# A hybrid attention layer on one core: sums of squares later, latent products earlier, the output product one block ahead

## The chip, the cores and the metric

The kernel runs on one core of one Trainium2 chip. The metric is the device time of one execution in microseconds (us), lower is better. TensorE (PE in the rows) does matmuls and transposes, with its weight loads apart (PEld); VectorE is DVE, ScalarE is ACT, GpSimd is POOL, and SyncE (SP) issues the DMAs.

## The reference, cut to what matters

```python
n = rms_norm(x, norm_g)                     # x: 2048 positions x 1024
dq, dk, dv, dgate, cq, ckv, kr, mgate = split(n @ w_in)
# group A: 4 heads, two softmax maps each
od = softmax(q1 k1) v - lam * softmax(q2 k2) v
od = rms_norm(od, subln_g) * (1 - lam_init) * silu(dgate)
# group B: 8 latent heads
q = rms_norm(cq, g) @ w_uq ; k, v = split(rms_norm(ckv, g) @ w_ukv)
om = causal_attention([q, rope], [k, rope], v) * silu(mgate)
h = x + concat(od, om) @ w_out
h = h + (p @ w_ple) * sigmoid(h @ w_ple_gate)
out = rms_norm(h, final_norm_g)
```

All inputs are float32, attention is causal, and rotary embedding is applied to parts of queries and keys.

## The kernel before, in words

Positions go in 16 blocks of 128 (`NB`) and 4 groups of 512 (`t`, `NT`). A float32 operand is split into two fp32r parts, high and low, and each product is three matmuls (high x high, high x low, low x high), so one 128-position block times 512 columns over a depth of 1024 is 24 matmuls. Work is written down by loops and reordered on each engine by a scheduler, with tile pools whose few buffers decide when a writer must wait. There are four stages.

**Input projection.** `load_x` (L213 and on) brings one of 8 row pieces of x for a group of 512 positions into a raw buffer (3 of them, shared with the weights), ScalarE writes the high part `xh` and the square `s1`, VectorE the low part `xl`, and GpSimd adds the squares into `sq` (the square of piece 0 writes it, L223; one buffer for all groups). `norms(t)` multiplies `sq` by ones into `pn` (8 small matmuls, L259), from which the scale `r_all` comes. The first pass over the 16 blocks makes the gates of group B: `mm_s` is the block's 24 matmuls into one of five PSUM tiles `ps`, `gate_evac` applies silu with the scale on ScalarE and stores the block. In block 0 of each group of four `norms` comes first, and the x of the next group is loaded two pieces per block.

**Latents.** `latent(b)` makes the 512 latent columns of a block, `turn` transposes them (`tpc`) into `cT`, and `up(t)` gives 12 products for a group of 512 positions: keys (3 matmuls), queries (9) and values (3) for each of four head pairs, 48 in all. Each is split by ScalarE and VectorE into one quarter of a ring `stage` and stored (128 x 1024 numbers) to `k_s`, `q_s` or `v_s`; the ring has four quarters, so a split waits until the store four products back has landed. From the ninth step on, each step of the loop does three products; what is left after the last step follows with two maxima of scores (`prep`, L171) for every product. The keys, values and queries of the first head pair are loaded back at named places of this loop, and the maxima need them.

**Latent attention, then differential attention.** The second has 4 heads x 8 pairs of blocks. `block` makes scores and exponentials (`pu`, `pb`), `weigh` transposes probabilities (one PSUM buffer `tpa`), ScalarE copies them (`ah`), they are multiplied by the values (`pod`), normed (`otd`), transposed and stored. Its loads (`load_out`) bring the output weights in pieces of 128 x 256, each with a cast on ScalarE and a subtraction on VectorE.

**Output.** For block b, from 15 down to 0: `mix` loads the gated attention `zg` (two loads and the gates, multiplied on GpSimd), `transpose_split` transposes and splits it (`zt4`), `p1` is the product with the output weights (48 matmuls), added to x; `p3` is the embedding product (12 matmuls); the sum is transposed (`ht4`) and multiplied by the gate weights into `p2` (48 matmuls). `load_split` brings the gate and embedding weights through two buffers `wr` at the start of this stage.

Of the kernel before, what the change touches and what calls it, by code (L numbers as in the profile page):

```python
# [8 lines left out]
F32 = mybir.dt.float32  # L9
F32R = mybir.dt.float32r  # L10
# [8 lines left out]
P = 128  # L19
S = 2048  # L20
D = 1024
KT = D // P
# [42 lines left out]
def tile_hymba(ctx, tc, a, out):  # L65
# [130 lines left out]
    with ExitStack() as c1:  # L196
# [138 lines left out]
        def gate_evac(b, pt, c0, w, g0):  # L335
            gt = ev.tile([P, 512], F32, name="gt", tag="e")
            A.activation(gt[:, :w], pt[:, c0:c0 + w], AF.Silu, scale=r_all[:, b:b + 1])
            nc.sync.dma_start(out=gate_s[b][:, g0:g0 + w], in_=gt[:, :w])

        for b in range(NB):  # L340
            if b == 3 * NB // 4:
                wn = load_w(1024, 512)
            pt = mm_s(b, *wg, 512)
            if b % 4 == 0:
                norms(b // 4)
            gate_evac(b, pt, 0, 512, 0)
# [205 lines left out]

            return [lambda pr=pr, f=f: f(pr) for pr in range(4) for f in (keys, queries, values)]

        turned, fresh, ups = 0, [], []
        for b in range(NB + 3):
            n = min(b, NB, max(0, 2 * (b - 3)))
            if b < NB:
                latent(b)
            for x in sorted(qns):  # L560
                q_turn(x)
            for x in fresh:
                q_rotary(x)
            fresh = list(range(turned, n))
            for x in fresh:
                turn(x)
            n_up = 3 if b >= 8 else 0
            for f in ups[:n_up]:
                f()
            if b in (12, 16):  # L570
                pair0[0].pop(0)()
            if b == NB:
                q0 = xpool.tile([P, 2, 2, 2, 512], F32R, name="q0", tag="vbig", bufs=2)
                for t in range(2):
                    load_q(0, t, q0[:, t])
                    maxes += [f for x in prep(0, t) for _, _, f in x]
                pair0[1].pop(0)()
                pair0[1].pop(0)()
            ups = ups[n_up:] + [f for t in range(turned // 4, n // 4) for f in up(t)]
            turned = n  # L580
        for i, f in enumerate(ups):
            f()
            for g in maxes[:2]:
                g()
            maxes = maxes[2:]
            if len(ups) - 1 - i == 12:
                pair0[0].pop(0)()
                pair0[1].pop(0)()
            if len(ups) - 1 - i == 9:
                pair0[0].pop(0)()  # L590
        for g in maxes:
            g()
        pair0[1].pop(0)()
# [214 lines left out]


    SC_D = 64.0 ** -0.5  # L810
    with ExitStack() as c3:
        sm = c3.enter_context(tc.tile_pool(name="p3m", bufs=4, reuse_waits="tile"))
        sb = c3.enter_context(tc.tile_pool(name="p3s", bufs=2, reuse_waits="tile"))
# [10 lines left out]
        def load_out():  # L824
# [13 lines left out]

            return [(0.3, lambda n=n: piece(n)) for n in range(4 * KT)]

        probs = {}

        def block(h, b):
# [8 lines left out]
            def unit(m, u):  # L852
                hd = heads[h]
                if m == 0 and u == 0:
                    st["s"] = sm.tile([P, 2, 2], F32, name="ssum", tag="ssum", bufs=4)
                if u == 0:
                    st[m] = pp.tile([P, S], F32, name="pb", tag=f"pb{m}", bufs=(6 if m == 0 else 2))
# [115 lines left out]
        for i, (h, g) in enumerate(order):  # L973
            if i % 8 == 0 and h < 3:
                pending = load_head(h + 1)
            if h == 3:
                pending, wload = pending + wload[:WN], wload[WN:]
            n = -(-len(pending) // max(1, HE - i % 8)) if h < 3 else len(pending)
            ld, pending = pending[:n], pending[n:]
            nxt = [x for y in blocks[LEAD + 2 * i:LEAD + 2 * i + 2] for x in block(*y)]  # L980
            if i == len(order) - 2:
# [3 lines left out]
            merge([(c, lambda x=(c, f): both.append(x)) for c, f in weigh(h, g)],  # L985
                  [(c, lambda x=(c, f): both.append(x)) for c, f in ld])
            merge(both, nxt)


    with ExitStack() as c4:  # L990
# [8 lines left out]
        turned = xpool.tile([P, 2, KT, P], F32R, name="turned", tag="vbig", bufs=2)  # L999
        wg, wl = [[], []], [[], []]  # L1000
        for k in range(KT):
            if k % 2 == 0:
                tg = dict(tag="vbig", bufs=2) if k >= 4 else dict(tag="big")
                w = xpool.tile([P, 2, 2, D], F32R, name="wg", **tg)
            for i in range(2):
                wg[i].append(w[:, k % 2, i])
        for i in range(2):
            for k in range(2):
                wl[i].append(wp.tile([P, D], F32R, name=f"wl{i}{k}"))

        def load_split(hi, lo, src, kts):
            for k in range(kts):
# [16 lines left out]
            return hi, lo  # L1029

        def product(pt, xh_, xl_, wh, wl, kts, nc_=2):
            for c in range(nc_):
                sl = slice(c * D // nc_, (c + 1) * D // nc_)
                for k in range(kts):
# [4 lines left out]
        st = {}  # L1039

        def load_mix(b):
            if b == NB - 1:
                zg = mixed[:, 0]
            else:
                zg = sb.tile([P, D], F32, name="zg", tag="zg")
                mix(b, zg, sb.tile([P, D], F32, name="gt4", tag="gt4", bufs=1))
            xr = sb.tile([P, D], F32, name="xr4", tag="xr4")
            nc.sync.dma_start(out=xr, in_=a["x"][b * P:(b + 1) * P, :])
            pr = sb.tile([P, 2, P], F32, name="pr4", tag="pr4", bufs=1)
            nc.sync.dma_start(out=pr, in_=a["pT"][:, b * P:(b + 1) * P].rearrange("(k p) s -> p k s", p=P))  # L1050
            ph = rp.tile([P, 2, P], F32R, name="ph4", tag="ph4")
            pl = rp.tile([P, 2, P], F32R, name="pl4", tag="pl4")
            V.tensor_copy(ph, pr)
            V.tensor_sub(pl, pr, ph.bitcast(F32))
            st[b] = zg, xr, ph, pl

        zh, zl = transpose_split(mixed[:, 0], "zt4", 2, (turned[:, 0], turned[:, 1]))
        load_mix(NB - 1)
        load_split(*wl, a["w_ple"], 2)
        load_split(*wg, a["w_gate"], KT)  # L1060
        nc.sync.dma_start(out=fg, in_=a["final_g"].partition_broadcast(P))
        for b in reversed(range(NB)):
            zg, xr, ph, pl = st.pop(b)
            if b > 0:
                load_mix(b - 1)
            p1 = ps.tile([P, D], F32, name="p1", tag="p4")
            product(p1, zh, zl, *wo, KT)
            for c in range(2):
                sl = slice(c * 512, (c + 1) * 512)
                V.tensor_add(xr[:, sl], p1[:, sl], xr[:, sl])  # L1070
            if b > 0:
                zh, zl = transpose_split(st[b - 1][0], "zt4", 2)
            p3 = ps.tile([P, D], F32, name="p3", tag="p4")
            product(p3, ph, pl, *wl, 2)
# [3 lines left out]
            product(p2, hh, hl, *wg, KT, parts)  # L1078
            sg4 = rg.tile([P, D], F32, name="sg4", tag="sg4")
            s4 = sb.tile([P, 4], F32, name="s44", tag="s44")  # L1080
            for c in range(parts):
# [60 lines left out]
```

## Time and profile before

| | |
|---|---|
| median of 3 runs | 2037.75 us (2037.64 to 2038.78) |
| the profiled execution | 2036.48 us, span 2034.7 us, mean granted TensorE clock 0.983 |
| TensorE busy | 1923.8 us (95%) |
| VectorE, ScalarE, GpSimd busy | 1223.9 (60%), 919.8 (45%), 503.9 us (25%) |
| first pass, latents, latent attention, differential attention, output (us of the span) | to 114, to 690, to 1155, to 1570, to 2035 |

TensorE is the engine that is nearly always busy; a busy share is an average over stages. The granted clock is 1.00 at 2.4 GHz and 0.5 at 1.2 GHz, so a stretch with 0.75 is half at one and half at the other. The first column of a timeline is the start in us from the span's start, the second the duration; matmuls overlap their neighbours, so their distance is read from starts.

### The profile page before, as it was taken

To read this page: it belongs to the slowest core of one execution; us is meant where nothing else is said; L and a number is where in the kernel's file an instruction comes from. 1 tells how busy PE (TensorE), PEld (TensorE's weight loads), DVE (VectorE), ACT (ScalarE), POOL (GpSimd) and SP (SyncE) were. 2 spreads that over 40 slices of the span, in tenths; PEclk is the share of its full clock that TensorE was granted. 3 is DMA by queue.
4 is the path that set the end of the run, shared out by engine and by line. 5 is a ranking of instruction groups with operands and counts; after the bars stand their busy time and mean duration, and the time that the engine had idled before them with its cause. 6 is when DMAs were issued, how large, how long until landed. Compare 5 with 4: busy or idle time off the path is not lost.

```text
span 2034.7 us, 28244 instructions
## 1 busy us (share of the span) xinstructions
PE 1923.8 (95%) x9521; PEld 1518.9 (75%) x9521; DVE 1223.9 (60%) x2749; ACT 919.8 (45%) x2089; POOL 503.9 (25%) x464
## 2 busy tenths in 40 slices
PE   8999999999999699999999989998988899999997
PEld 5788878898887477777777667776766687777786
DVE  5353677632446487888888688777886523333322
ACT  4422101122333467677767676777786311111111
POOL 4400345300000166666656400000011201111100
PEclk9999999999998899999999999999999999999999
DMA  5442333322167643524141311531022522222210
GB/s 166 140 149 87 130 126 135 120 87 77 63 209 254 225 129 105 142 55 131 36 109 51 93 43 39 151 113 33 16 81 78 185 90 68 88 88 88 76 47 21
DMA packets 171681, 209.74 MB, mean 103 GB/s; under 512 B 38876, under 2 KB 99180, under 8 KB 171536
## 3 DMA queue, kind: packets, MB, share of 16 engines
q1 hardware_dynamic: 171536, 207.93, 32.7%
q8 instruction: 75, 1.23, 0.3%
q14 instruction: 70, 0.57, 0.1%
HBM read 129.65 MB, written 78.14 MB: 102 GB/s over the span
## 4 chain that ended last, share of the span: by engine, by line
PE 76%; DVE 7%; ACT 7%; DMA 4%; issue 2%; POOL 2%; SPq 1%; ACTq 0%; POOLq 0%; DVEq 0%
PE p L1035 6%; PE p L1037 6%; PE p L1036 6%; PE ps L252 5%; PE ps L253 5%; PE ps L251 5%; PE pod L936 3%; PE pm L171 3%; PE po L704 3%; PE pst L675 3%; PE po L705 3%; PE pst L673 3%; PE pst L674 3%; PE ps L372 3%; PE ps L370 3%; PE ps L371 3%
## 5 line engine op out<-in xcount | busy, mean ns | idle before, releaser
L690 POOL TENSOR_TENSOR acc<-ph,acc 128x512 f32<-128x512 f32 (+3 forms) x208 | 216.7, 1042 | 164.5 <-DVE acc L685 75.8
L251 PE MATMUL ps<-wh,xh 128*128 128x512 f32 (+1 forms) x640 | 229.5, 359 | 9.3 <-DVE wh L240 8.2
L252 PE MATMUL ps<-wl,xh 128*128 128x512 f32 (+1 forms) x640 | 227.8, 357 | 0.5 <-DVE wl L241 0.4
L253 PE MATMUL ps<-wh,xl 128*128 128x512 f32 (+1 forms) x640 | 227.2, 357 | 0.4 <-DVE xl L228 0.3
L678 ACT ACTIVATE ph<-pst 128x512 fp32r<-128x512 f32 (+1 forms) x320 | 170.3, 532 | 114.1 <-PE pst L675 61.9
L695 DVE TENSOR_TENSOR pl<-pst,ph 128x512 fp32r<-128x512 f32 (+1 forms) x320 | 193.3, 607 | 45.6 <-ACT pst L679 42.8
L107 POOL TENSOR_TENSOR s<-s,half 128x2 f32<-128x2 f32 (+1 forms) x48 | 31.9, 664 | 648.2 <-DVE s L106 552.5
L872 DVE TENSOR_REDUCE mxd<-pu 128x1 f32<-128x1024 f32 (+4 forms) x192 | 173.0, 909 | 21.7 <-PE pu L871 14.8
L883 ACT ACTIVATE pb<-pu,nm 128x1024 f32<-128x1024 f32 (+4 forms) x192 | 165.3, 866 | 27.2 <-DVE nm L878 16.9
L679 ACT ACTIVATE pst<-pst 128x512 f32<-128x512 f32 (+1 forms) x320 | 168.9, 528 | 0.0
L868 PE MATMUL pu<-hd 128*128 128x512 f32 (+3 forms) x320 | 141.3, 442 | 21.2 <-ACT pb L883 19.1
L251 PEld LDWEIGHTS ps<-wh,xh 128*128 128x128 f32 x640 | 121.6, 190 | 29.6 <-ACT sq L223 6.5
L936 PE MATMUL pod<-ah,hd 128*128 128x256 f32 (+1 forms) x576 | 141.6, 370 | 0.5 <-ACT ah L928 0.5
L173 DVE TENSOR_REDUCE mx<-pm 128x1 f32<-128x512 f32 x192 | 130.0, 680 | 15.1 <-PE pm L171 15.0
L253 PEld LDWEIGHTS ps<-wh,xl 128*128 128x128 f32 x640 | 121.7, 190 | 19.7 <-DVE xl L228 2.0
L252 PEld LDWEIGHTS ps<-wl,xh 128*128 128x128 f32 x640 | 121.7, 190 | 19.0 <-DVE wl L241 1.6
L1084 DVE TENSOR_TENSOR sg<-p,sg 128x512 f32<-128x512 f32 (+1 forms) x34 | 20.8, 655 | 175.5 <-ACT sg L1083 175.5
L704 PE MATMUL po<-ph,vall 128*128 128x512 f32 (+1 forms) x320 | 117.8, 374 | 4.2 <-ACT ph L678 4.0
L869 PE MATMUL pu<-hd 128*128 128x512 f32 (+3 forms) x320 | 121.7, 386 | 0.0
L673 PE MATMUL pst<-QH,kall 97*128 97x512 f32 (+2 forms) x296 | 119.1, 402 | 0.0
L171 PE MATMUL pm<-kall,QH 96*128 96x512 f32 (+3 forms) x296 | 115.2, 404 | 3.9 <-DVE mx L173 2.5
L705 PE MATMUL po<-pl,vall 128*65 128x512 f32 (+1 forms) x320 | 115.4, 363 | 0.0
(263 smaller groups left out, 4620.8 us busy)
## 6 DMA issues: line engine op xcount, KB each, us to landing
hd<-dq_s SPq DMA_DIRECT2D x192, 128.0 KB
wr<-in_w_in SPq DMA_DIRECT2D x40, 256.0 KB
xr<-in_xT SPq DMA_DIRECT2D x32, 256.0 KB
dq_s<-th SPq DMA_DIRECT2D x32, 256.0 KB
dq_s<-tl SPq DMA_DIRECT2D x32, 256.0 KB
k_s<-stage SPq DMA_DIRECT2D x16, 512.0 KB
q_s<-stage SPq DMA_DIRECT2D x16, 512.0 KB
v_s<-stage SPq DMA_DIRECT2D x16, 512.0 KB
```

Of the source, the lines that this page charges most:

```text
L171: T.matmul(pm[:, :w], lhsT=q, rhs=keys_of(pr, e, c)[0][0:96, :w], start=True, stop=True)
L251: T.matmul(pt[:, :w], lhsT=h, rhs=wh[k][:, :w], start=(k == 0), stop=False)
L252: T.matmul(pt[:, :w], lhsT=h, rhs=wl[k][:, :w], start=False, stop=False)
L253: T.matmul(pt[:, :w], lhsT=l, rhs=wh[k][:, :w], start=False, stop=(k == KT - 1))
L673: T.matmul(pt[:, o:], lhsT=kh[0:97], rhs=qh[0:97, o:], start=True, stop=False)
L678: A.activation(ph[:, o:], pt[:, o:], AF.Exp, scale=SC_M)
L690: eng.tensor_add(self.acc[:, o:], ph[:, o:].bitcast(F32), self.acc[:, o:])
L695: V.tensor_sub(pl[:, o:], pt[:, o:], ph[:, o:].bitcast(F32))
L704: T.matmul(self.po[:, o:], lhsT=vv[:, 0:128], rhs=ph[:, o:], start=(kc == 0), stop=(kc == self.n - 1))
L705: T.matmul(self.po2[:65, o:], lhsT=vv[:, 64:129], rhs=pl[:, o:], start=(kc == 0), stop=False)
L872: V.reduce_max(st["x", m][:, u:u + 1], pu[:, :w], axis=AX.X)
L936: T.matmul(st["po"][:, o:], lhsT=vv, rhs=st[u][:, i, o:], start=(kc == 0), stop=(kc == nk - 1))
```

## The change

First pass: `norms` moves from the first to the third block of each group, and the products of three blocks are held in PSUM until then, to be evacuated together. Latents: four products per step from the seventh step on, in place of three from the ninth, with the loads of the first pair by a count of products, and three maxima per product. Differential stage: the rows of x of the last block, its gated attention and that of block 14 are brought in, transposed there (`turn_z`), the last block's output product (`top_part`, 48 matmuls) is made in the score tiles, and half of the gate weights are loaded in 16 pieces of 128 x 256 (`load_gate`); the `pb` buffers of map 0 go from 6 to 5. Output: the output product of a block is made one block earlier (`add_z`), and only the other half of the gate weights is loaded in this stage.

```diff
+        held = []
         for b in range(NB):
...
-            pt = mm_s(b, *wg, 512)
-            if b % 4 == 0:
+            held.append((b, mm_s(b, *wg, 512)))
+            if b % 4 == 2:
                 norms(b // 4)
-            gate_evac(b, pt, 0, 512, 0)
+            if b % 4 >= 2:
+                for x, pt in held:
+                    gate_evac(x, pt, 0, 512, 0)
+                held = []
...
+        def run_up():
+            nonlocal done
+            ups.pop(0)()
+            done += 1
+            if done == 27:
+                pair0[0].pop(0)()
+            if done == 38:
+                pair0[1].pop(0)()
+            if done == 39:
+                pair0[0].pop(0)()
+            for g in maxes[:3]:
+                g()
+            del maxes[:3]
...
-            n_up = 3 if b >= 8 else 0
-            for f in ups[:n_up]:
-                f()
-            if b in (12, 16):
-                pair0[0].pop(0)()
...
+            for _ in range(min(len(ups), 4 if b >= 6 else 0)):
+                run_up()
+            if b in (12, 14):
+                pair0[0].pop(0)()
...
+        while ups:
+            run_up()
...
+        def load_gate(k2):
...
+                nc.sync.dma_start(out=ws, in_=a["w_gate"][(2 * k2 + k) * P:(2 * k2 + k + 1) * P, sl])
+                A.copy(w[:, k, 0, sl], ws)
+                V.tensor_sub(w[:, k, 1, sl], ws, w[:, k, 0, sl].bitcast(F32))
...
+        def turn_z(b, g, to):
+            tp = ps_t.tile([P, 4, P], F32, name="tpz", tag="tpa")
+            for j in range(4):
+                k = 4 * g + j
+                T.transpose(tp[:, j], side["zg", b][:, 0, k * P:(k + 1) * P], ident)
+            split_ps(to[:, 0, 4 * g:4 * g + 4], to[:, 1, 4 * g:4 * g + 4], tp)
+
+        def top_part(c, k0, n):
...
+                T.matmul(o, lhsT=z[:, 0, k], rhs=wh, start=(k == 0), stop=False)
+                T.matmul(o, lhsT=z[:, 0, k], rhs=wl, start=False, stop=False)
+                T.matmul(o, lhsT=z[:, 1, k], rhs=wh, start=False, stop=(k == KT - 1))
+            if k0 + n == KT:
+                V.tensor_add(top[:, sl], o, top[:, sl])
...
+            if i == len(order) - 5:
+                lay(NB - 1, top)
+            if i == len(order) - 4:
+                turned = make_z()
+                side["z"] = turned[:, 0]
+                more = [(0.45, lambda g=g: turn_z(NB - 1, g, turned[:, 0])) for g in range(2)]
+            if i == len(order) - 3:
+                lay(NB - 2, None)
+                more = [(1.4, lambda k=k: top_part(0, k, 2)) for k in range(0, KT, 2)]
             if i == len(order) - 2:
-                mixed = xpool.tile([P, 2, D], F32, name="mixed", tag="vbig", bufs=2)
-                mix(NB - 1, mixed[:, 0], mixed[:, 1])
+                pending = pending + load_gate(0) + load_gate(2)
+                more = [(1.4, lambda k=k: top_part(1, k, 2)) for k in range(0, KT, 2)]
+                more += [(0.45, lambda g=g: turn_z(NB - 2, g, turned[:, 1])) for g in range(2)]
...
+        load_split(*wl, a["w_ple"], range(2))
+        zg = load_z(NB - 3)
+        load_split(*wg, a["w_gate"], range(2, 4))
+        add_z(NB - 2, (turned[:, 1, 0], turned[:, 1, 1]))
+        load_split(*wg, a["w_gate"], range(6, KT))
...
+            if 1 < b < NB - 1:
+                add_z(b - 1, zn)
...
             hh, hl = transpose_split(xr, "ht4", 1)
-            p2 = ps.tile([P, D], F32, name="p2", tag="p4")
+            if 0 < b < NB - 1:
+                embed()
+                if b > 1:
+                    zn = transpose_split(zg, "zt4", 2)
             parts = 2 if b > 0 else 4
             product(p2, hh, hl, *wg, KT, parts)
```

How this moves instructions shows at three places. On ScalarE in the first pass, where the second group's x is brought in (`sq` is the Square of its first piece, `s1` that of another piece, `gt` a gate evacuation, `xh1` a high part), the rows before are:

```order
L223 ACTIVATE sq_351<-xr_348 128x512
L337 ACTIVATE gt_343<-ps_311,r_all_162 128x512
L226 ACTIVATE s1_357<-xr_354 128x512
L337 ACTIVATE gt_386<-ps_361,r_all_162 128x512
L226 ACTIVATE s1_392<-xr_389 128x512
L220 ACTIVATE xh1_346<-xr_396,norm_g_150 128x512
L226 ACTIVATE s1_399<-xr_396 128x512
L337 ACTIVATE gt_428<-ps_403,r_all_162 128x512
```

and with the change:

```order
L226 ACTIVATE s1_347<-xr_344 128x512
L226 ACTIVATE s1_379<-xr_376 128x512
L223 ACTIVATE sq_341<-xr_338 128x512
L220 ACTIVATE xh1_336<-xr_383,norm_g_150 128x512
L226 ACTIVATE s1_386<-xr_383 128x512
L337 ACTIVATE gt_422<-ps_311,r_all_162 128x512
L337 ACTIVATE gt_425<-ps_351,r_all_162 128x512
L337 ACTIVATE gt_428<-ps_390,r_all_162 128x512
```

Three evacuations stand together behind the Square, and the squares of later pieces ahead of it. On TensorE at the last transposition of latents (`tpc`), before (products by `uk`, `uqh` with `cT2` are those of the third group of positions, `cT3` of the fourth):

```order
L468 MATMUL tpc_5646<-ident_149,cx_5548 128x128 x4
L523 MATMUL ps_5653<-cT2_4997,uk00_4330 128x512
L524 MATMUL ps_5653<-cT2_4997,uk00_4330 128x512
L525 MATMUL ps_5653<-cT2_4997,uk01_4331 128x512
L532 MATMUL ps_5660<-cT2_4997,uqh_4328 128x512
```

and with the change:

```order
L472 MATMUL tpc_5770<-ident_149,cx_5665 128x128 x4
L481 MATMUL ps_5813<-ur_4306,cT3_5473 128x256
L482 MATMUL ps_5813<-ur_4308,cT3_5473 128x256
L527 MATMUL ps_5831<-cT3_5473,uk00_4330 128x512
L536 MATMUL ps_5848<-cT3_5473,uqh_4328 128x512
L549 MATMUL ps_5880<-uk10_4332,cT3_5473 128x512
```

The products behind the last transposition are now the fourth group's: 36 of the 48 stand ahead of it, where 24 did. On TensorE at the end of the differential stage (`pod` and `pzd` are its last head's), before:

```order
L936 MATMUL pod_16831<-ah_16833,hd_14611 128x256
L936 MATMUL pod_16831<-ah_16833,hd_14611 128x128
L946 MATMUL pzd_16843<-ident_149,otd_16841 128x128 x2
L1027 MATMUL tp4_16895<-ident_149,mixed_16761 128x128 x4
L1027 MATMUL tp4_16902<-ident_149,mixed_16761 128x128 x4
L1035 MATMUL p1_17003<-wo_15821,turned_16885 128x512
```

and with the change:

```order
L888 MATMUL tpz_16879<-ident_149,mixed_16372 128x128 x4
L1003 MATMUL pod_16818<-ah_16842,hd_14615 128x256
L1003 MATMUL pod_16818<-ah_16842,hd_14615 128x128
L1118 MATMUL p1_17093<-wo_15825,turned_16528 128x512
L1119 MATMUL p1_17093<-wo_15825,turned_16528 128x512
L1013 MATMUL pzd_16890<-ident_149,otd_16888 128x128 x2
L1120 MATMUL p1_17093<-wo_15825,turned_16528 128x512
L1118 MATMUL p1_17093<-wo_15825,turned_16528 128x512
L1119 MATMUL p1_17093<-wo_15825,turned_16528 128x512
```

Block 14's transposition (`tpz`) and its output product `p1` stand among the last products of the differential stage, where its end and the transposition of the last block's row stood one behind the other.

## Rows read from the trace of the kernel before

**Rows 1.** the page, busy time of each engine and its share

```profile
PE 1923.8 (95%) x9521; PEld 1518.9 (75%) x9521; DVE 1223.9 (60%) x2749; ACT 919.8 (45%) x2089; POOL 503.9 (25%) x464
```

**Rows 2.** windows: stretch and length, busy us of engines (instructions), clock, DMA share, GB/s

```profile
30.00:100.00 70.00, 65.59 (x277) 50.73 (x276) 22.11 (x29) 35.32 (x58) 34.22 (x26) 0.95 0.48 144
650.00:690.00 40.00, 26.12 (x86) 18.30 (x85) 18.21 (x42) 9.22 (x19) 0.00 (x0) 0.76 0.74 264
1560.00:1585.00 25.00, 20.20 (x87) 15.35 (x88) 8.28 (x28) 10.26 (x32) 4.63 (x5) 0.86 0.61 197
1585.00:1651.00 66.00, 58.12 (x249) 45.43 (x248) 31.08 (x48) 20.22 (x37) 10.44 (x8) 0.95 0.44 147
1651.00:2000.00 349.00, 345.18 (x1571) 277.21 (x1570) 116.03 (x189) 58.13 (x126) 36.45 (x34) 1.00 0.22 73
```

**Rows 3.** waits of TensorE, 30 to 115: total us, times, longest

```profile
PE pn L259 <- POOL sq L227: 2.9, 3, 1.9
```

**Rows 4.** timeline of TensorE in the first pass: start, duration

```profile
49.79 0.63 PE L251 MATMUL ps<-wh,xh 128*128 128x512 f32 x1
...
51.93 0.60 PE L253 MATMUL ps<-wh,xl 128*128 128x512 f32 x1
...
69.60 1.05 PE L259 MATMUL pn<-ones,sq 128*128 128x1 f32 x8 [0.29 <-POOL sq L227]
...
96.81 0.63 PE L251 MATMUL ps<-wh,xh 128*128 128x512 f32 x1
...
99.80 0.56 PE L252 MATMUL ps<-wl,xh 128*128 128x512 f32 x1
```

**Rows 5.** timeline of TensorE in a steady output block

```profile
1731.68 0.39 PE L1037 MATMUL p<-wo,zt4l 128*128 128x512 f32 x1
...
1733.08 0.40 PE L1037 MATMUL p<-wo,zt4l 128*128 128x512 f32 x1
```

**Rows 6.** chain of waits, 30 to 115: start, duration

```profile
35.53 4.45 DMA xr<-in_xT
```

**Rows 7.** waits of TensorE, 640 to 705

```profile
PE ps L523 <- DVE stage L111: 6.4, 1, 6.4
```

**Rows 8.** timeline of TensorE, the last transposition of latents

```profile
623.48 0.60 PE L468 MATMUL tpc<-ident,cx 128*128 128x128 f32 x4
```

**Rows 9.** waits of ScalarE, 640 to 705

```profile
ACT stage L110 <- DMA k_s<-stage: 11.3, 2, 8.3
```

**Rows 10.** chain of waits, 625 to 705

```profile
664.09 0.57 SPq L189
...
671.63 3.55 DMA k_s<-stage
...
680.64 4.91 DMA v_s<-stage
...
689.91 0.59 ACT stage L110
```

**Rows 11.** waits of TensorE, 1554 to 1573

```profile
PE pzd L946 <- ACT otd L941: 2.4, 2, 1.7
```

**Rows 12.** chain of waits, 1585 to 1652

```profile
1597.42 6.45 DMA wr<-in_w_gate
```

**Rows 13.** timeline of TensorE, transpositions of three output blocks and a following matmul

```profile
1618.18 1.03 PE L1027 MATMUL tp<-ident,zg 128*128 128x128 f32 x8
...
1650.61 1.04 PE L1027 MATMUL tp<-ident,zg 128*128 128x128 f32 x8
...
1678.08 1.03 PE L1027 MATMUL tp<-ident,zg 128*128 128x128 f32 x8
1678.87 0.48 PE L1035 MATMUL p<-wl,ph 128*128 128x512 f32 x1
```

**Rows 14.** line 836: min/median/max duration in ns, first and last start in us

```profile
L836 ACT CAST wo<-ws x32: 405/410/443, 1463.8 to 1539.3; 128x256 fp32r<-128x256 f32 x32
```

**Rows 15.** waits of TensorE, 1652 to 2010

```profile
PE p L1035 <- ACT ht4h L110: 3.8, 13, 0.3
```

More of the change, by code (lines that the diff above doesn't have):

```diff
@@ L986, in tile_hymba @@
                   [(c, lambda x=(c, f): both.append(x)) for c, f in ld])
+            if more:
+                work, both = both, []
+                merge([(c, lambda x=(c, f): both.append(x)) for c, f in work],
+                      [(c, lambda x=(c, f): both.append(x)) for c, f in more])
             merge(both, nxt)
@@ L998, in tile_hymba @@
         wo = [[wt[k // 2][:, k % 2, i] for k in range(KT)] for i in range(2)]
-        turned = xpool.tile([P, 2, KT, P], F32R, name="turned", tag="vbig", bufs=2)
         wg, wl = [[], []], [[], []]
[L1001 to L1006, printed above, removed]
+        for k2 in range(KT // 2):
+            if k2 not in gates:
+                tg = dict(tag="vbig", bufs=2) if k2 >= 2 else dict(tag="big")
+                gates[k2] = xpool.tile([P, 2, 2, D], F32R, name="wg", **tg)
+            for k in range(2):
+                for i in range(2):
+                    wg[i].append(gates[k2][:, k, i])
         for i in range(2):
@@ L1011, in load_split @@
         def load_split(hi, lo, src, kts):
-            for k in range(kts):
+            for k in kts:
                 wr = rg.tile([P, D], F32, name="wr4", tag="sg4")
@@ L1031, in product @@
         def product(pt, xh_, xl_, wh, wl, kts, nc_=2):
+            ks = (0, 1, 4, 5, 2, 3, 6, 7) if kts == KT else range(kts)
             for c in range(nc_):
                 sl = slice(c * D // nc_, (c + 1) * D // nc_)
-                for k in range(kts):
+                for k in ks:
                     T.matmul(pt[:, sl], lhsT=xh_[:, k], rhs=wh[k][:, sl], start=(k == 0), stop=False)
@@ L1037, in product @@
                     T.matmul(pt[:, sl], lhsT=xl_[:, k], rhs=wh[k][:, sl], start=False, stop=(k == kts - 1))
[L1039 to L1048, printed above, removed]
+        rows, zs, emb = {NB - 1: top}, {}, {}
@@ L1049, in load_mix, with load_rows, load_z, load_emb @@
+        def load_rows(b):
+            rows[b] = sb.tile([P, D], F32, name="xr4", tag="xr4", bufs=2) if (NB - 1 - b) % 3 else top
+            nc.sync.dma_start(out=rows[b], in_=a["x"][b * P:(b + 1) * P, :])
+        def load_z(b):
+            zg = sb.tile([P, D], F32, name="zg", tag="zg", bufs=2)
+            mix(b, zg, rg.tile([P, D], F32, name="gt4", tag="sg4"))
+            return zg
+        def load_emb(b):
             pr = sb.tile([P, 2, P], F32, name="pr4", tag="pr4", bufs=1)
             nc.sync.dma_start(out=pr, in_=a["pT"][:, b * P:(b + 1) * P].rearrange("(k p) s -> p k s", p=P))
-            ph = rp.tile([P, 2, P], F32R, name="ph4", tag="ph4")
@@ L1061, in tile_hymba, with add_z @@
[L1061 to L1065, printed above, removed]
+            emb[b] = ph, pl
+        def add_z(b, z):
             p1 = ps.tile([P, D], F32, name="p1", tag="p4")
-            product(p1, zh, zl, *wo, KT)
+            product(p1, *z, *wo, KT)
             for c in range(2):
                 sl = slice(c * 512, (c + 1) * 512)
[L1070 to L1074, printed above, removed]
+                V.tensor_add(rows[b][:, sl], p1[:, sl], rows[b][:, sl])
@@ new lines, in tile_hymba, with embed @@
+        load_rows(NB - 2)
+        load_emb(NB - 1)
+        load_split(*wl, a["w_ple"], range(2))
+        zg = load_z(NB - 3)
+        load_split(*wg, a["w_gate"], range(2, 4))
+        nc.sync.dma_start(out=fg, in_=a["final_g"].partition_broadcast(P))
+        add_z(NB - 2, (turned[:, 1, 0], turned[:, 1, 1]))
+        load_split(*wg, a["w_gate"], range(6, KT))
+        for b in reversed(range(NB)):
+            xr = rows[b]
+            if b > 1:
+                load_rows(b - 2)
+            if 1 < b < NB - 1:
+                add_z(b - 1, zn)
+            if b == 0:
+                add_z(0, zn)
+            p3, p2 = (ps.tile([P, D], F32, name=n, tag="p4") for n in ("p3", "p2"))
+            def embed():
+                product(p3, *emb.pop(b), *wl, 2)
+                if b > 0:
+                    load_emb(b - 1)
+            if b == 0:
+                embed()
@@ L1075, in tile_hymba @@
             hh, hl = transpose_split(xr, "ht4", 1)
-            p2 = ps.tile([P, D], F32, name="p2", tag="p4")
+            if 0 < b < NB - 1:
+                embed()
+                if b > 1:
+                    zn = transpose_split(zg, "zt4", 2)
             parts = 2 if b > 0 else 4
             product(p2, hh, hl, *wg, KT, parts)
+            if b == NB - 1:
+                embed()
+                zn = transpose_split(zg, "zt4", 2)
+            if b > 2:
+                zg = load_z(b - 3)
```

56 lines of the change are left out of this document (36 added, 20 removed).

## The prediction, made before the change was run

> **What bounds the kernel now.** I read the page first: TensorE is busy for 1923.8 of 2034.7 us [rows 1], so the whole room for a reordering is 111 us of idle TensorE, and what it runs at half clock. The windows say where that room lies. The stretch to read beside all others is the steady output stage: 345.18 of 349 us busy at clock 1.00 [rows 2], with a 512-column matmul starting every 0.233 us (six steps from 1731.68 to 1733.08) [rows 5]. Measured by that, three stretches are poor [rows 2]: the first pass (65.59 of 70 us), the end of the latent stage (26.12 of 40 us at 0.76), and the seam between differential and output stage (20.20 of 25 us at 0.86, then 58.12 of 66 us at 0.95). The waits in each tell what ends last there. The change touches exactly these and the steady blocks; it removes almost no instruction, so it is worth what it closes of these gaps.
>
> **First pass: sums two blocks later.** Each of four groups multiplies the sums of squares by ones (`pn`); in three of them TensorE waited for GpSimd's sum, 2.9 us together [rows 3]. Behind two groups it ran at half clock (1.2 GHz instead of 2.4): six matmuls from 49.79 to 51.93 and eight from 96.81 to 99.80, 0.43 us apart instead of 0.233 [rows 4], so 14 x 0.2 = 2.8 us. With `pn` two blocks (some 11 us) later the sum is there, and the half-clock runs, which stood behind those waits alone, go too: 2.9 + 2.8 = 5.7 us. The upper bound is all that the window lost: 277 matmuls, of them 32 for `pn`; 245 x 0.233 = 57.1, and four groups at 1.05 [rows 4] make 61.3 of 70, so 8.7. The lower bound is 0, if the wait only moves. I take **-5.7**. What is late next: `sq` is one buffer, and ScalarE's Square of the next x waits for `pn`; three gate evacuations now stand right behind it, before the copies of the next x. An x load took 4.45 us from issue to landing [rows 6]. From `pn` to the first matmul that wants the last of these rows are two blocks, 48 x 0.233 = 11.2 us; a raw buffer that comes free some 4.6 us after `pn` (Square and three evacuations at about 0.65 us each, and the copies between), the load and the copy take about 9. The margin is 2 us a group.
>
> **Latent stage: four products per step, from the seventh block.** At the last latent transposition, at 623.48 [rows 8], 24 of 48 products are still to do; the order now leaves 12. TensorE pays for the 12 that moved with 12 x 5 matmuls x 0.233 = 14 us (a key, query and value product have 3, 9 and 3), so the last latent comes at about 637.5. Behind it, SyncE issues and stores bound the stretch: TensorE waits 6.4 us for the stage ring [rows 7], ScalarE 11.3 us for the key stores that free the ring [rows 9], and the chain runs SP issue, store 3.55 us, store 4.91 us [rows 10]. From 623.5 to the last ring copy at 689.9 pass 66 us [rows 8, 10]. A product leaves 128 x 1024 numbers of 4 bytes, 0.524 MB, so twelve fewer are 6.3 MB less behind the last latent; at the 264 GB/s of that window [rows 2] that is 23.8 us. Net 14 - 23.8 = -9.8; since the loads of the next stage keep their place and their issue time (0.57 us each, some of them in a row [rows 10]), I take **-9**. Bounds: 0 (the stream doesn't shorten, TensorE only does the same work earlier) and -20 (all that this window lost, 40 - 86 x 0.233).
>
> **Seam between the stages.** In 1560 to 1585 TensorE is idle for 4.8 us, at 0.86: with 0.14 x 25 for the clock some 8 us lost; it waits for ScalarE's copies in the last heads' tail [rows 11]. In 1585 to 1651 it issued 249 matmuls; at the steady stage's 1571 in 349 us these need 55.3 of the 66 us, so 10.7 lost: gate weights arrive through two buffers (a piece lands 6.45 us after issue [rows 12]), and blocks last 32.4 us where a steady one lasts 27.5 [rows 13]. Together 19 us. The change puts the 48 matmuls of the last block's output product and part of block 14's between the tail's dependent ones, so idle time there is filled, and it loads four of eight gate weights before the stage begins; six row loads are left for the two buffers instead of ten. At 6.45 us for two of them they are in about 20 us after the stage begins, and the first gate product needs the last at about 23: 8.7 of the 10.7 go. In the tail I count 3.3 of 8 won, because it now also carries 16 pieces at 0.41 us on ScalarE [rows 14] and as much on VectorE, and four more passes through the one transpose buffer. Sum **-12**. Bounds -3 (only the idle time filled) and -19.
>
> By the rows, pieces of 128 KB cost ScalarE 0.41 us each [rows 14], and the DMA side has room: the tail's window moves 197 GB/s where the latents' end reaches 264 [rows 2]. The Trainium skill, "DMA: Bandwidth & Descriptors", section "Bandwidth", speaks against them: it wants transfers of at least 1 MiB for three quarters of the peak rate and shows 64 KB at a third of it. By its table 2 MB in such pieces would be (an estimate) some 20 us of transfers instead of 12; with all 8 us on the path the seam would give -4 and the kernel 2015. No row here prices that alone.
>
> **Steady blocks.** Every output block waits 0.3 us for ScalarE's split of the transposed residual, 13 times, 3.8 us [rows 15]. The output product one block ahead lets the residual be added long before its transposition, and the 12 embedding matmuls (2.8 us) cover the split: **-3.8**. Bounds: +2 (three products share the PSUM buffers in a new order) and -9 (13 x 0.7: a block's 27.47 us less 108 x 0.233 and two sets of transposes at 0.79 from their start to the next matmul's [rows 13]). The end behind the last matmul is not touched.
>
> **Sum.** -5.7 - 9 - 12 - 3.8 = -30.5 against the profiled execution's 2036.5: 2006.0. The median of the runs stands 1.3 us above that execution, so **2007 us**.
>
> **Rivals.**
> 1. *The latent stream doesn't shorten* (0.13). For: SP issues one load every 0.6 us and stands idle little there [rows 10]; the next stage's query and value loads need buffers that the last latent holds. Against: ScalarE waits for stores, not loads [rows 9]. Then the latent term is between 0 and +14 instead of -9: 2016 to 2030.
> 2. *The seam's tail grows* (0.14). ScalarE is what the tail waits for [rows 11], and it gets 16 more casts (6.6 us), VectorE 16 subtractions, the transpose buffer four more turns at some 2 us. Then the tail gives its filling back and the weights' early load is paid there: -3 instead of -12, 2016. (The rule of the Trainium skill, "DMA: Bandwidth & Descriptors", on small transfers points the same way, at 2015.) Against: only the last pass carries them, and the moved matmuls wait for none of it.
> 3. *The late sums hold up the next x* (0.06, the other side). One `sq` buffer and one queue: the copies of rows 5 to 7 of the next x wait behind `pn` and three evacuations. If a row's load takes 6.5 us instead of the 4.45 seen [rows 6], or its buffer comes free later, each of three groups begins to wait, at most 11.2 us each: +33.6 instead of -5.7, 2046. It turns the whole change slower from (24.8 + 4.1) / 3 = 9.6 us a group on.
> 4. *The change doesn't do what it says*, because the scheduler moves work on its own: for the seam and the steady blocks the order shows the moved matmuls where they are wanted, so this is only the case of steady blocks already at their floor: +3.8, 2011, inside the forecast's range.
>
> **How the numbers follow.** The forecast (all four terms within about half of their size, 1995 to 2015) gets 0.64, the rivals 0.13, 0.14 and 0.06; 0.03 is left for two of them together and for what I don't see. A range from 1994 to 2026 leaves out rival 3, half of the double cases, and gains above 43 us, together less than 0.2. A measurement of this kernel tells 0.2%, 4.1 us, from no change: faster 0.91 (rivals 1 and 2 are still faster), same 0.03, slower 0.06.
>
> **What would show it.** In the new profile: no wait of `pn` for `sq` and clock 1.00 from 30 to 115 us; if rival 3 holds, instead waits of `ps` for x copies two blocks behind each `pn`. The last latent transposition near 637 and the last ring copy near 681 instead of 689.9; if rival 1 holds, at 690 or later, with stores landing well before ScalarE asks. At the seam: TensorE busy over 0.9 from 1530 on, the first output blocks within 1 us of the steady 27; if rival 2 holds, ScalarE's casts on the chain there. In steady blocks no wait for `ht4h`. The forecast is wrong if a stretch that is not named here changes by over 3 us, or if the total gain lies under 20 us.

## The result, and the profile after

The changed kernel takes 2008.88 us (median, 2006.62 to 2010.07) where the kernel before takes 2037.70 on the same chip: ratio 0.9857, 95% interval 0.9840 to 0.9874, so 26 to 33 us faster. The forecast was 2007. The profiled executions differ by 29.9 us of span (2034.7 and 2004.8), and the rest of this text splits those.

The page of the changed kernel, busy time of the engines (as [rows 1]):

```profile
span 2004.8 us, 28293 instructions
...
PE 1909.7 (95%) x9521; PEld 1513.0 (75%) x9521; DVE 1217.5 (61%) x2757; ACT 919.4 (46%) x2097; POOL 501.5 (25%) x464
```

TensorE still is 95% busy: of the 29.9 us only 16 are idle time (111 before, 95 now); its busy time fell by 14 us with the same 9521 instructions. By the mean clocks (0.983 and 0.987) it stood at half clock for some 69 us before and 52 now, which is some 8.5 us less of busy time (an estimate, since the clocks are rounded); the steady output blocks, whose matmuls start at a better pace (below), give most of the rest.

Windows of the changed kernel (stretch and length, busy us of each engine, clock, DMA share, GB/s), which answer to [rows 2]; the later ones are shifted by what was won before them:

```profile
30.00:100.00 70.00, 68.75 (x305) 54.64 (x304) 24.81 (x28) 33.19 (x55) 34.05 (x25) 1.00 0.48 143
636.00:676.00 40.00, 28.30 (x113) 20.18 (x111) 24.24 (x73) 8.72 (x19) 0.00 (x0) 0.81 0.79 258
1564.00:1573.00 9.00, 5.95 (x30) 3.93 (x30) 4.23 (x13) 4.13 (x14) 0.70 (x1) 1.00 0.18 55
1573.00:1581.00 8.00, 8.00 (x38) 6.57 (x37) 3.80 (x12) 2.88 (x10) 0.70 (x1) 1.00 0.82 253
1581.00:1592.00 11.00, 7.18 (x33) 4.95 (x32) 5.96 (x10) 3.98 (x7) 1.38 (x2) 1.00 0.94 306
1620.00:1970.00 350.00, 350.00 (x1611) 284.44 (x1610) 110.89 (x196) 59.47 (x131) 35.00 (x35) 1.00 0.23 78
```

The first pass issues 305 matmuls in the 70 us where it issued 277, all at 1.00. The latents' end still is poor (0.81 where it was 0.76), and the seam still has two holes: 3 us in the differential stage's tail and 3.8 us at the start of the output stage. The steady output stage has no idle time left.

Its timeline on TensorE at the end of the first pass, the last two latent transpositions, the first score, the first differential score (`pu`) and the transposition of block 13's residual:

```profile
107.27 0.27 PE L296 MATMUL rtp<-ident,r_all 128*16 128x128 f32 x1
...
629.95 0.60 PE L472 MATMUL tpc<-ident,cx 128*128 128x128 f32 x4
...
635.78 0.60 PE L472 MATMUL tpc<-ident,cx 128*128 128x128 f32 x4
...
671.11 0.77 PE L685 MATMUL pst<-q,kall 97*128 97x512 f32 x1 [5.66 <-issue]
...
1147.03 0.45 PE L935 MATMUL pu<-hd 128*128 128x128 f32 x1 [0.82 <-DVE zt L739]
...
1641.46 0.71 PE L1109 MATMUL tp<-ident,xr 128*128 128x128 f32 x5
```

and the same points of the kernel before (here the truly last transposition, which [rows 8] missed by one):

```profile
114.42 0.27 PE L296 MATMUL rtp<-ident,r_all 128*16 128x128 f32 x1
...
628.65 0.60 PE L468 MATMUL tpc<-ident,cx 128*128 128x128 f32 x4
...
685.82 0.47 PE L673 MATMUL pst<-q,kall 97*128 97x512 f32 x1 [3.71 <-issue]
...
1160.66 0.30 PE L868 MATMUL pu<-hd 128*128 128x128 f32 x1 [0.83 <-DVE zt L727]
...
1654.24 0.49 PE L1027 MATMUL tp<-ident,xr 128*128 128x128 f32 x3
```

A stage's own share is the difference of its distances between such points. The first pass ends 7.1 us earlier. From there to the first score it was 571.4 us and is 563.8: the latents gave 7.6. For the seam I compare the transposition of block 13's residual (1654.24 before, 1641.46 after), less 8.4 us because the changed kernel has at that point done one output product more and one embedding product less (36 matmuls at 0.233). From the first differential score (1160.7, 1147.0) that is 493.5 and 486.1: the seam gave 7.5. From there to the end it was 380.5 and is 371.7: 8.7 for the steady blocks. Some 1 us was given back in the latent attention between; what took it stays open.

| term | predicted | measured |
|---|---|---|
| first pass | -5.7 | -7.1 |
| latents | -9 | -7.6 |
| seam | -12 | -7.5 |
| steady blocks | -3.8 | -8.7 |
| sum | -30.5 | -29.9 with the 1 us given back |

### The profile page after: what moved, and what is told of

The parts are those of the page before. It is cut to its first block, busy times and chain, and to the rows that moved or that the text cites. A ratio compares the mean times of both kernels' runs of the same rounds, so it can differ in the third digit from the quotient of the medians.

```text
span 2004.8 us, 28293 instructions
## 1 busy us (share of the span) xinstructions
PE 1909.7 (95%) x9521; PEld 1513.0 (75%) x9521; DVE 1217.5 (61%) x2757; ACT 919.4 (46%) x2097; POOL 501.5 (25%) x464
## 4 chain that ended last, share of the span: by engine, by line
PE 77%; DVE 7%; ACT 7%; DMA 3%; issue 3%; POOL 1%; SPq 1%; ACTq 0%; POOLq 0%; DVEq 0%
PE p L1118 6%; PE p L1120 6%; PE p L1119 6%; PE ps L252 5%; PE ps L251 5%; PE ps L253 5%; PE pod L1003 3%; PE pm L171 3%; PE po L716 3%; PE pst L687 3%; PE po L717 3%; PE pst L685 3%; PE pst L686 3%; PE ps L376 3%; PE ps L375 3%; PE ps L374 3%
## 5 line engine op out<-in xcount | busy, mean ns | idle before, releaser
L717 PE MATMUL po<-pl,vall 128*65 128x512 f32 (+1 forms) x320 | 115.5, 363 | 0.0
```

The costliest lines, as they stand in the source:

```text
L717: T.matmul(self.po2[:65, o:], lhsT=vv[:, 64:129], rhs=pl[:, o:], start=(kc == 0), stop=False)
```

## The experiments

Points in the trace of every kernel, in us: end of the first pass; last latent transposition; first score of the latent attention; the seam as above (first differential score to block 13's residual, less 8.4 where the new order holds); the span; and the ratio to the kernel before on the same chip.

| kernel | pass | last latent | first score | seam | span | ratio (95%) |
|---|---|---|---|---|---|---|
| before | 114.4 | 628.7 | 685.8 | 493.5 | 2034.7 | 1 |
| changed | 107.3 | 635.8 | 671.1 | 486.1 | 2004.8 | 0.9857 (0.9840 to 0.9874) |
| again | 107.6 | 636.0 | 671.8 | 485.9 | 2005.2 | 0.9859 (0.9846 to 0.9873) |
| e1_late_sums | 108.3 | 623.6 | 681.4 | 492.8 | 2030.9 | 0.9964 (0.9951 to 0.9977) |
| e2_latents | 115.5 | 643.9 | 679.8 | 495.4 | 2031.9 | 0.9965 (0.9952 to 0.9978) |
| e6_sums_last | 111.6 | 641.1 | 677.3 | 485.6 | 2009.9 | 0.9874 (0.9844 to 0.9903) |
| e10_sums_second | 107.8 | 636.3 | 672.0 | 484.2 | 2003.3 | 0.9862 (0.9848 to 0.9875) |
| e7_three | 107.1 | 628.6 | 681.1 | 486.1 | 2009.8 | 0.9869 (0.9849 to 0.9889) |
| e8_rows_act | 109.7 | 637.7 | 673.2 | 485.3 | 2005.5 | 0.9861 (0.9848 to 0.9875) |
| e3_neither | 107.9 | 636.6 | 672.5 | 483.8 | 2003.7 | 0.9857 (0.9842 to 0.9871) |
| e4_gates_late | 108.1 | 636.9 | 672.7 | 490.8 | 2011.6 | 0.9898 (0.9883 to 0.9912) |
| e5_top_late | 108.0 | 636.8 | 673.3 | 483.5 | 2004.2 | 0.9858 (0.9841 to 0.9874) |
| e9_z_first | 107.2 | 635.5 | 671.5 | 488.9 | 2008.2 | 0.9877 (0.9862 to 0.9891) |
| e11_best | 107.2 | 635.8 | 671.8 | 481.3 | 1999.7 | 0.9839 (0.9825 to 0.9852) |

Unchanged code scatters by 1 to 2 us at each point: the pass ends at 107.1 to 108.3 in eight of the nine kernels with the changed first pass, and at 109.7 in one; the seam is 484.2 to 486.1 in the six whose seam is that of the changed kernel, and 492.8 to 495.4 in the three that have the old one.

**The unaltered kernel once more.**

> The changed kernel once more, unaltered, on the chip of the three runs beside it, so that differences of 2 us can be told from differences between chips. All theories: 0.9857 of the kernel before, within 0.002.

2006.49 us, 0.9859: as expected.

**First pass: the late sums alone, and the sums one block later and one earlier.** `e1_late_sums` is the kernel before with this:

```diff
-            if b % 4 == 0:
+            if b % 4 == 2:
                 norms(b // 4)
```

and the held evacuations of the change; the other two are the changed kernel with `== 3` and `== 1` (evacuations from that block on).

> The kernel before with the late sums alone. Theory (a wait costs what the distance between matmul starts says, more than the wait row): first pass ends at 107.3 us as in the changed kernel, 7.1 us earlier than before, total -7 us, about 2030.7. Rival (the prediction's sizing by the wait rows and the half-clock matmuls): -5.7, pass ends at 108.7.

> The changed kernel with the sums of squares in the fourth block of a group instead of the third, and all four gates evacuated there. Theory (the copies of the next x stand behind them, with no margin left): matmuls wait for x copies some 8 to 11 us in each of three groups, +25 to +34 us over the changed kernel, first pass ends at 132 to 141. Rival (a margin remains): waits under 1 us more, total within 3 us of the changed kernel.

> The changed kernel with the sums of squares in the second block of a group instead of the third. Theory (the longest wait for a sum was 1.9 us, so one block, 5.6 us, is enough, and the copies of the next x have a block more): no wait for the sum, none for x copies, first pass 1 to 2 us shorter than the changed kernel's, total -1 to -2. Rival (one block isn't enough on this chip): waits for sums and half clock come back, +2 to +6.

Alone the late sums give 0.36% (0.23 to 0.49), 7 us, and the pass ends 6.1 us earlier: the theory by distances of starts, 7.1, and the prediction's 5.7 lie both within the scatter. In the trace of before the reading by starts gives more than the wait row: to the three late `pn` groups the distances are 1.14, 0.68 and 2.33 us where 0.233 is the pace, 3.45 lost, where the row says 2.9 [rows 3].

With the sums in the fourth block both sides of the expectation fell (the total is 3.5 us above the changed kernel's by the ratios, 5.1 in the trace), the theory by far. Waits of TensorE in that first pass (30 to 118 us; total us, times, longest):

```profile
PE ps L253 <- DVE xl L228: 1.9, 3, 0.7
PE ps L251 <- ACT xh L220: 1.6, 1, 1.6
PE rtp L296 <- POOL r_all L107: 1.1, 1, 1.1
```

The copies of the next x are late by 1.9 us in one group (`xl`) and by 1.6 in another (`xh`), not by 8 to 11 in each of three. The three rows add up to 4.6 us where the changed kernel waits 1.2, and the pass ends 4.3 later; the last row is new, since the last scales are now wanted right behind `pn`, and eight matmuls at half clock follow it. With the sums in the second block there is no wait for a sum either, and the pass is no shorter: TensorE still waits for x copies, 1.6 us for `xh` and 0.6 for `xl`. The kernel before waited 1.1 and 0.3 for them, so they don't stand behind the late sums. One block, 5.6 us, would have been enough.

**Latents: alone, with three products per step, and with another queue.** `e2_latents` is the kernel before with the latent stage's part of the change. The other two edits, on the changed kernel:

```diff
-            for _ in range(min(len(ups), 4 if b >= 6 else 0)):
+            for _ in range(min(len(ups), 3 if b >= 6 else 0)):
```

```diff
-                nc.sync.dma_start(out=QH[pr, t, e][96:97,
+                (nc.scalar if pr == 0 and t < 2 else nc.sync).dma_start(out=QH[pr, t, e][96:97,
```

> The kernel before with the latent stage's change alone. Theory (the stores behind the last latent shrink by 21 us, TensorE pays 14): last transposition of latents 7 us later than before minus the first pass's gain, so near 643, last ring copy near 683 instead of 689.9, total -6.7 us, about 2031. Rival (prediction): -9, about 2028.7. Rival (stream is bound by issues and loads): 0 or slower.

> The changed kernel with three latent products per step from the seventh step, instead of four. Theory (what counts is how early the stream of stores begins, and a step's products only have to be done before the next group's): within 2 us of the changed kernel. Rival (four per step are what shortens the stream): the last ring copy comes 3 to 6 us later, total +3 to +6.

> The changed kernel with the 16 small transfers of the negated maxima into the first pair's queries issued from ScalarE's queue instead of SyncE's. Theory (stores and loads bound the end of the latents, 258 GB/s, and the issue time is only the order in which they go): last ring copy within 1.5 us of the changed kernel, total within 1.5 us. Rival (SyncE's issue time of about 0.6 us each is on the chain: 16 x 0.6): last ring copy 4 to 9 us earlier, total -4 to -9.

Alone: 0.35% (0.22 to 0.48), 7 us; from the end of the first pass to the first score 564.3 us where it was 571.4. The theory's -6.7 holds, and the prediction's -9 lies inside the interval too (4.5 to 9.8 us); the rival that the stream doesn't shorten falls.

Three per step leave 30 products ahead of the last transposition, not 36 as I had assumed. The kernel is 5.0 us slower in the trace and 2.4 by the ratios, nearer to the rival than to the theory. With 24, 30 and 36 products ahead the last transposition comes 514.2, 521.5 and 528.5 us behind the first pass: 1.19 us a product, against 5 x 0.233 = 1.17 worked out. The last copy into the ring comes 575.5, 572.6 and 568.4 us behind it: on average 0.6 us earlier for every product moved. In the changed kernel (timeline of ScalarE):

```profile
675.68 0.58 ACT L110 CAST stage<-ps 128x512 fp32r<-128x512 f32 x1 [2.75 <-DMA q_s<-stage]
```

So a product less behind the last latent shortens the stream there by 1.8 us, which for 0.524 MB is some 290 GB/s (an estimate). Up to the ring copy the trade is near to linear, but what follows is not: with 30 products ahead the first score stands 573.9 us behind the pass, later than before (571.4), since TensorE waits 10.9 us there for the last split into the ring, and the first differential score comes after 1045.2 us, against 1046.2 before and 1039.8 with 36. Why six products gain 1 us there and twelve 6.4 stays open.

With ScalarE's queue for the 16 small transfers the first score stands 35.5 us behind the last transposition, 35.3 to 35.8 in the changed kernel's two traces: SyncE's issue time is not what bounds it, though the last ring copy comes 2 us sooner, a little more than the theory's 1.5. The stores are what is left: in the changed kernel ScalarE still waits for all three kinds (its waits, 640 to 676):

```profile
ACT stage L110 <- DMA q_s<-stage: 5.9, 2, 3.1
...
ACT stage L110 <- DMA k_s<-stage: 3.1, 1, 3.1
ACT stage L110 <- DMA v_s<-stage: 2.9, 1, 2.9
```

11.9 us together, against 20.3 before (640 to 705), of which the keys had 11.3 [rows 9].

**The seam: each part put back.** In `e5_top_late` the last block's product stands at the start of the output stage, in `e4_gates_late` all gate weights are loaded there, and `e3_neither` has both there. The product's edit (for the weights the line with `load_gate(0) + load_gate(2)` goes, and `load_split` takes all eight):

```diff
-                more = [(1.4, lambda k=k: top_part(0, k, 2)) for k in range(0, KT, 2)]
...
+        add_z(NB - 1, (turned[:, 0, 0], turned[:, 0, 1]))
         add_z(NB - 2, (turned[:, 1, 0], turned[:, 1, 1]))
```

> The changed kernel with neither gate weights nor the last block's output product in the differential stage; both stand at the start of the output stage, and the output product stays one block ahead. Theory (steady blocks are worth 0.72 each, by the distance of starts, and the seam the rest): steady blocks 26.9 us as in the changed kernel, the seam 5 to 9 us longer than there, total +5 to +9. Rival (prediction: steady 3.8, seam 12): +12, and steady blocks the same 26.9.

> The changed kernel without gate weights in the differential stage, all eight loaded in the output stage; the last block's output product stays early. Theory (the early weights are the seam's gain): +8 to +14 us. Rival (the filled idle time is the gain): +0 to +4.

> The changed kernel with the last block's output product at the start of the output stage; gate weights stay early. Theory (its 48 matmuls cost their whole 11 us in the differential stage and filled no idle time there, while at the start of the output stage they cover loads): -3 to +1 us. Rival (prediction: they fill idle time of the tail): +3 to +8.

The seam is 486.1 us with both early, 490.8 with late weights, 483.5 with the late product, 483.8 with neither. So weights loaded early are worth some 5 us if the product is early as well, and nothing that shows (0.3) if it isn't; the product early costs 2.5 (2.9 between `e10_sums_second` and `e11_best`, which differ in it alone). In the whole time `e4_gates_late` is 8 us slower than the changed kernel by the ratios, at the lower end of its theory, 6.8 in the trace; `e5_top_late` is level with it, inside its theory. For `e3_neither` both sides, +5 to +9 and +12, were wrong: leaving both out loses nothing (0.9857 in both, and a seam 2.3 us shorter); its steady blocks take 26.9 us, as expected.

Where the 5 us go can be seen in `e4_gates_late`. It comes to the transposition of block 15's residual at 1580.66, the changed kernel at 1580.82; but its first cast of a gate weight starts at 1590.07, and TensorE has nothing to do (its waits, 1572 to 1630):

```profile
PE tp L1108 <- POOL zg L819: 8.0, 1, 8.0
```

The wait is put down to block 13's row, which came first; the gate products follow right behind it. In the changed kernel gate and embedding products fill most of that time.

The last transposition of the differential stage (`pzd`) divides the seam into the stage's tail and the start of the output stage. Before:

```profile
L946 PE MATMUL pzd<-ident,otd x64: 270/272/476, 1170.1 to 1569.2; 128*128 128x128 f32 x64
```

in the changed kernel:

```profile
L1013 PE MATMUL pzd<-ident,otd x64: 270/272/329, 1157.1 to 1572.9; 128*128 128x128 f32 x64
```

and with the late product:

```profile
L1013 PE MATMUL pzd<-ident,otd x64: 270/272/328, 1159.7 to 1568.2; 128*128 128x128 f32 x64
```

From the first differential score that is 425.9 and 418.8 us, 408.5 before. The edit moves 48 matmuls, but the scheduler moves others back across `pzd`: 62 matmuls of output products stand ahead of it in the changed kernel, 34 with the late product. The 28 between them take 6.5 us at full pace and cost 7.1 in the tail, so no idle time there hid them; behind `pzd` the same 28 cost 4.5, so there 2.0 are hidden. Against the kernel before, with 0.233 us for each matmul and 0.79 for each eight transpositions that changed sides, each kernel gained (us; the sums are the seam's gains to 0.1):

| kernel | output matmuls ahead of `pzd` | in the tail | at the start of the output stage |
|---|---|---|---|
| before | 0 | | |
| changed: both early | 62 | -1.4 | 8.9 |
| e4_gates_late | 62 | 0.7 | 2.0 |
| e5_top_late | 34 | -0.8 | 10.9 |
| e3_neither | 32 | 0.1 | 9.6 |

By the scatter above, the tail gave nothing that shows in any of them. All four transpose the rows of blocks 15 and 14 in the tail and load them early; no run takes that back.

**The seam's remaining hole.** At 1591.94 the changed kernel waits for GpSimd's product of block 13's row (waits of TensorE, 1582 to 1630):

```profile
PE tp L1109 <- POOL zg L819: 2.8, 2, 2.3
```

`e9_z_first` moves that row's loads two lines up:

```diff
+        zg = load_z(NB - 3)
         load_split(*wl, a["w_ple"], range(2))
-        zg = load_z(NB - 3)
```

> The changed kernel with block 13's attention row and its gates issued ahead of the embedding weights at the start of the output stage. Theory (TensorE waits 2.8 us for GpSimd's product of that row, which comes late because its gates take a buffer behind the embedding weights): that wait goes, total -1 to -3 us. Rival (the embedding weights come later by as much): wait for their cast instead, 0 to +2.

The wait goes, and another, longer one takes its place (the same window):

```profile
PE p L1118 <- ACT wl L1098: 3.3, 2, 2.7
```

The seam grows by 2.8 us (the whole time by 4 by the ratios), more than even the rival said: the row's gates and the weights share two buffers, and whichever comes second is late.

**Both improvements together.** The sums in the second block, the product late:

> The changed kernel with the sums of squares in the second block and the last block's output product at the start of the output stage (gate weights stay early). Theory (both gains add: 1 to 2 us in the first pass, 2.6 at the seam, by the trace of the run that moved the product alone): -3 to -5 us against the changed kernel on the same chip. Rival (the seam's 2.6 us were between chips): -1 to -2.

2002.58 us (2001.48 to 2003.43) beside 2006.49 (2005.77 to 2008.49) for the changed kernel on the same chip, and 0.9839 (0.9825 to 0.9852) of the kernel before: this beats both. The gain is at the seam alone (481.3; the first pass ends at 107.2, as in the changed kernel). It is 2 us more than in `e5_top_late`, which differs only in the first pass; by as much the seam of `e10_sums_second` is shorter than the changed kernel's, which again differs only there. So 2 us may be the scatter of the seam, or come from the first pass in a way that no run shows.

## Why the prediction was right, point by point

**First pass**: right in mechanism. No wait for `sq` is left, and the clock is 1.00; 7.1 where 5.7 was forecast, and 6.1 in `e1_late_sums`. The wait row counts from the modelled end of the last matmul: by starts the three waits are 3.45 us, so 0.55 was missing from the term; the rest of the difference lies within the scatter. The margin of "2 us a group" was wrong in its working: with one block less than the change leaves, `e6_sums_last` waits 3.5 us for x copies in all. Its step "three gate evacuations now stand right behind it, before the copies of the next x" had left out that the scheduler moves copies ahead, of which one (`xh1`) can be seen in the change's own rows above. So rival 3 had its price wrong: even a block further the pass gets 4.3 us longer, not 33.6.

**Latents**: right, with its price. "24 of 48 products are still to do" was paired with the last transposition but one (623.48 instead of 628.65), which cancelled, since both ends moved: 14 us more for the twelve products were 14.3 (528.5 - 514.2), and 23.8 us less of stream were 21.4 (from the last transposition to the last ring copy 61.3 us before, 39.9 after). The forecast -9 against -7.6 at the first score. Rival 1 is excluded by `e2_latents` and `e8_rows_act`.

**Seam**: -7.5 where -12 was forecast; one step came out and one failed. "8.7 of the 10.7 go" at the start of the output stage was 8.9, and without the early weights 6.9 of these go (`e4_gates_late`). But the early weights are not the only way to it: where a second output product stands ahead of the first gate product, the start gains 9.6 without them. And what was lost there before was read too narrowly. Of 7.8 us of TensorE's waits in the kernel before (1585 to 1652), 1.9 were for gate weights:

```profile
PE tp L1027 <- issue: 2.8, 1, 2.8
PE tp L1027 <- DVE zt4l L111: 1.7, 2, 1.0
PE p L1035 <- ACT wg L1016: 1.5, 1, 1.5
PE p L1035 <- ACT ht4h L110: 1.4, 1, 1.4
PE p L1036 <- DVE wg L1017: 0.4, 1, 0.4
```

The first two rows, 4.5 us, stand ahead of transpositions of residuals, and in the changed kernel no such wait is left. The step that failed is "in the tail I count 3.3 of 8 won": the moved matmuls cost their whole time there, and the tail gained nothing (-1.4). The sign for it, TensorE busy over 0.9 from 1530 on, failed too: 53.4 of 62 us to 1592. Rival 2 had this half right. What the changed kernel's tail waits for is the split of block 14's row, in the one transpose buffer (waits of TensorE, 1535 to 1575):

```profile
PE tpa L991 <- DVE turned L111: 2.6, 2, 1.3
```

The small pieces did no harm that shows: with 16 of them the late product's seam is 483.5, with pieces of 256 KB at the output stage 483.8. The rule of the Trainium skill, "DMA: Bandwidth & Descriptors", section "Bandwidth", would by the prediction's estimate have brought the kernel to 2015; no run here shows such a loss, and none prices the pieces alone.

**Steady blocks**: right in mechanism, the term too small by more than half. A block now takes 26.89 us (eleven of them from 1641.46 to 1937.29) instead of 27.6. In the kernel before, around the transposition of the residual:

```profile
1709.12 0.40 PE L1037 MATMUL p<-wl,pl 128*128 128x512 f32 x1
1709.36 1.04 PE L1027 MATMUL tp<-ident,xr 128*128 128x128 f32 x8
1710.69 0.50 PE L1035 MATMUL p<-wg,ht4h 128*128 128x512 f32 x1 [0.29 <-ACT ht4h L110]
1711.03 0.40 PE L1036 MATMUL p<-wg,ht4h 128*128 128x512 f32 x1
```

and in the changed kernel, where another transposition stands before the gate product:

```profile
1698.86 1.04 PE L1109 MATMUL tp<-ident,zg 128*128 128x128 f32 x8
1699.66 0.48 PE L1118 MATMUL p<-wg,ht4h 128*128 128x512 f32 x1
1699.97 0.39 PE L1119 MATMUL p<-wg,ht4h 128*128 128x512 f32 x1
```

The row says that 0.29 us were idle. From the transposition's start to the next matmul's it is 1.33 us against 0.80, so the wait cost 0.53, and the matmuls behind it start 0.34 us apart where 0.31 and 0.233 follow now; a block gains 0.72. The step "13 times, 3.8 us" took the wait row as the cost; my own upper bound, 13 x 0.7 by starts, was the right sum (8.7). No wait of TensorE is left between 1630 and 1980. No run takes this term back alone; `e3_neither`, with neither early part, keeps its 26.89.

The errors of the four terms are 1.4 too little, 1.4 too much, 4.5 too much and 4.9 too little; that they cancel to within 1 us is luck. Each measured term lies inside the bounds that the prediction gave it, the steady blocks' only by 0.3.

## What to carry to other kernels

Price a wait on TensorE by the distance between starts, against the same pair without a wait, and not by the idle time in the wait row: waits of 0.29 us in the row cost 0.45 and 0.53 here, one of 1.94 cost 2.1. Before loading weights early for the start of a stage, see whether independent products can stand there instead: either covered the loads (8.9 and 9.6 us gained there), and both together were little better (10.9). And where work is moved ahead of a point that waits for a stream of stores, count both sides per item: here 1.2 us paid and 1.8 us saved for each product, up to the end of that stream.

## What the runs showed that was not expected

A wait alone didn't bring the half clock in the first pass. In the changed kernel TensorE waits 0.71 us for an x copy (1.12 us between starts) and goes on at full clock; in `e6_sums_last` and `e10_sums_second` it does so even behind 1.6 us. Before, 0.66 us ahead of the eight one-column matmuls of `pn` was followed by six matmuls at 0.43 us, and 0.29 us ahead of them by none [rows 4]; in `e6_sums_last` 1.1 us ahead of a transposition that stands two matmuls behind `pn` was followed by eight. Why, no run here settles.
